# Attention fills of two transformer blocks dealt to other places, and the value product one head later

## The chip, the cores and the metric

The kernel runs on one core of one Trainium2 chip. Its time is the device time of one execution in microseconds. Three runs of the kernel before took 2408.8 to 2412.59 us, with a median of 2411.03 us. Everything below about waits and durations comes from one further execution that a hardware profiler recorded.

## The reference: two blocks over 512 tokens

The input is 512 tokens of width 1024. Block 1 conditions on a vector `c`, runs two kinds of attention side by side, and then looks experts up; block 2 is a transformer layer with 16 extra tokens. Everything is float32. Cut to what the change touches:

```python
def first_block(...):                      # DEPTH = 1
    mod = (silu(c) @ w_ada + b_ada).reshape(b, 6, d)         # six rows of 1024
    shift1, scale1, gate1, shift2, scale2, gate2 = ...
    hn = rmsnorm(x, norm1_g) * (1 + scale1) + shift1
    qa, ka, va, qi, ki, wi, qb, kb, vb, ga, gb = split(hn @ w_in)
    ya = dsa_attention(qa, ka, va, qi, ki, wi, rel_bias)     # 8 heads, top 128 keys by an index score, bias by distance
    yb = stick_breaking_attention(qb, kb, vb)                # 8 heads
    merged = sigmoid(ga) * (ya @ w_proj_a) + sigmoid(gb) * (yb @ w_proj_b)
    x = x + gate1 * (merged @ w_out)
    hn2 = rmsnorm(x, norm2_g) * (1 + scale2) + shift2
    x = x + gate2 * peer_ffn(hn2, ...)
    return rmsnorm(x, final_g)

def _layer(...):                           # block 2
    a_out = forgetting_attention(q, k, v, cum_logf)          # 8 heads
    p_out = pooled @ w_pool * pool_scale                     # 4 groups
    h = h + concat(a_out, p_out) @ w_out
    n2 = rmsnorm(h, norm2_w)
    return h + (silu(n2 @ w_gate) * (n2 @ w_up)) @ w_down
```

## The kernel before

Each float32 product is built from three products of rounded parts: every operand is split into a high part and the remainder, and `mm3` (L177 to L179) issues high by high, low by high, and high by low. A weight chunk is loaded by one 512 KB transfer on the queue SP (`raw`, L168), copied to `whi` on ScalarE (L171) and subtracted to `wlo` on VectorE (L172). Every split on VectorE is one subtraction (`hilo`, L243, L246).

The program text is handed to a framework that puts each engine's instructions into one order from its own estimate of when they are ready; an engine then works through its order and waits at the first instruction whose inputs are missing. The order of the text therefore matters less than where an item is offered, and a tile's memory can be given to its next user only when the last reader is done.

Block 1's attention has two stages. In the first (pool `pb`) the eight stick-breaking heads run: `sb_z` computes a head's scores and softplus parts, `sb_t` multiplies them with a triangular matrix (L645, L646) and leaves the weights `ah` and `al`, and `pv` multiplies these with the values (L413, L414), after which `head_sum` (L447, L448) adds the parts into `yb`. In the second (pool `pa`) the eight index-selected heads run: `da_s` with the softmax (L762 to L766), `transpose_p` (TensorE transposes L777, split into `pth` and `ptl`), and `pv` and `head_sum` again, into `ya`. Before these two stages an index stage forms the score tiles `iacc1` to `iacc3`.

Other work is dealt into 32 slots, two per head, by the table `B1F`: slots 0 to 15 belong to the first stage, 16 to 31 to the second. One letter is one item:

- `k`: a query or key projection for one pair of heads: 24 matmuls of 512 columns, one `whi`, one `wlo`, and two split subtractions (`dup`, `stk`).
- `g`: a gate projection: 24 matmuls, one `whi`, one `wlo`.
- `v`: the value projection of the second stage: 192 matmuls of 256 columns, four `wlo`, eight small split subtractions.
- `t`: a step of the top-128 search, alternately `MAX8` and `MATCH_REPLACE8` on `iacc` (L592, L593).
- `a`: half of one of the rows of `silu(c) @ w_ada` that are not needed at the start. Four transfers of 512 KB (`adaraw`, L300, in two buffers) are multiplied by the condition and summed by eight VectorE instructions into `adaacc` (L286, L288). A matmul with a vector of ones then sums over partitions (L305, the tile is 128x512 and the matmul is float32, which appears as two matmul records), VectorE adds a bias row (L308), for two of the eight halves also scales it (L311), and a 2 KB transfer writes the row to `modrow` in DRAM (L312).

The bias table of the second stage is made between the index stage and the first heads: `rb` and `oh` are loaded (L542, L543), multiplied (L547), negated into `rs` (L548), written to DRAM (`rdr`, L549) and spread to `r128` (L551). These tiles lie in a pool `pr` that opens when the index stage's pool closes.

After the heads come `w_proj_a` and `w_proj_b` (eight column blocks, 406 to 496 us), `w_out` with the second normalisation (to about 570 us), then the expert part, which the change does not touch. Block 2's eight heads (1890 to 1990 us) have a table of their own, `B2F`, of eleven slots; its letters are column blocks of the u projection (a to d), pooling sums (e to h), pooling products (A to D), the second half of q and v, and four blocks of the pooled half of `w_out` (W to Z). Its `w_out` for the attention half runs row block by row block; after each of four, `done` adds it to `x`, normalises (`xn`, L1452) and transposes it into `n2h` and `n2l` (`rows_out`, L235). The feed-forward starts with `gemm_halves`: four products over the first 256 tokens, then over the last 256.

Of the kernel before, what the change touches and what calls it, by code (L numbers as in the profile page):

```python
# [11 lines left out]
F32 = mybir.dt.float32  # L12
# [15 lines left out]
H = 8  # L28
# [43 lines left out]
class Kern:  # L72
# [207 lines left out]
    def ada_acc(self, acc, raws, cond):  # L280
        nc = self.nc
        for kc in range(0, KC, 2):
            raw = raws(kc)
            for j in range(2):
                if kc + j == 0:
                    nc.vector.tensor_scalar(acc, raw[:, 0], cond[:, 0:1], None, op0=ALU.mult)  # L286
                else:
                    nc.vector.scalar_tensor_tensor(acc, raw[:, j], cond[:, kc + j:kc + j + 1], acc,  # L288
                                                   op0=ALU.mult, op1=ALU.add)

    def ada(self, pool, cond, col, dst_row, half, gain=None):
        nc, I = self.nc, self.I
        wv = I["w_ada"].rearrange("(k p) n -> p k n", p=128)
        if True:
            c0 = col * D + half * 512

            def raws(kc):
                raw = pool.tile([128, 2, 512], F32, tag="adaraw", bufs=ADB, name=self.nm("adaraw"))
                with self.tc.issue_after(self.loaded):
                    nc.sync.dma_start(raw, wv[:, kc:kc + 2, c0:c0 + 512])  # L300
                return raw
            acc = pool.tile([128, 512], F32, tag="adaacc", bufs=1, name=self.nm("adaacc"))
            self.ada_acc(acc, raws, cond)
            p = self.psg()
            nc.tensor.matmul(p, lhsT=self.onesf, rhs=acc, start=True, stop=True)  # L305
            bro = pool.tile([1, 2, 512], F32, tag="adab", bufs=1, name=self.nm("adab"))
            nc.sync.dma_start(bro[:, 0], I["b_ada"][0:1, c0:c0 + 512])
            nc.vector.tensor_tensor(bro[:, 0], p[0:1], bro[:, 0], op=ALU.add)  # L308
            if gain is not None:
                nc.sync.dma_start(bro[:, 1], I[gain][0:1, half * 512:half * 512 + 512])  # L310
                nc.vector.scalar_tensor_tensor(bro[:, 0], bro[:, 0], 1.0, bro[:, 1], op0=ALU.add, op1=ALU.mult)  # L311
            nc.sync.dma_start(self.modrow[dst_row:dst_row + 1, half * 512:half * 512 + 512], bro[:, 0])  # L312
# [143 lines left out]
    def block1(self):  # L456
# [40 lines left out]
        with tc.tile_pool(name="pidx", bufs=1) as pi:  # L497
            pva = pat_ctx.enter_context(tc.tile_pool(name="pva", bufs=1, side="right"))
            pad = pat_ctx.enter_context(tc.tile_pool(name="pad", bufs=1, side="right"))
            adas = fillers([(lambda c=c, r=r, g=g, hf=hf: self.ada(pad, cond, c, r, hf, g))  # L500
                            for c, r, g in ((2, 0, None), (4, 1, "norm2_g"), (3, 2, None), (5, 3, None)) for hf in range(2)])
# [19 lines left out]
            acc = {b: b1.tile([128, 128 * (b + 1)], F32, name=f"iacc{b}") for b in range(1, 4)}  # L521
            for pr in range(4):
# [58 lines left out]
        fill = {"g": fillers([gate_fill(n, j) for n in range(4) for j in range(2)]), "a": adas, "v": va_fill,  # L581
# [29 lines left out]


# [23 lines left out]
        def sb_t(pool, st):  # L636
            zs, sph, spl = st
            ahs, als = [], []
            for s in range(TB):
# [9 lines left out]
                ah = pool.tile([128, n], F32R, tag=f"ah{s}", name=self.nm("ah"))  # L649
                al = pool.tile([128, n], F32R, tag=f"al{s}", name=self.nm("al"))  # L650
# [6 lines left out]
        with tc.tile_pool(name="pb", bufs=1) as pb:  # L657
            cur = sb_z(pb, 0)
            for h in range(H):
                fills(2 * h)  # L660
                nxt = None
# [931 lines left out]
```

## Time and profile before

| | |
|---|---|
| median of three runs | 2411.03 us (2408.8 to 2412.59) |
| profiled execution, its own time | 2410.34 us |
| span from the first to the last instruction | 2408.5 us |
| TensorE busy / VectorE busy / ScalarE busy | 96% / 72% / 43% |
| mean granted TensorE clock, share of full speed | 0.981 |
| chain that ended last: TensorE / VectorE / DMA / ScalarE | 86% / 7% / 2% / 2% |

The span is 1.84 us shorter than the execution's own time; that remainder lies around it and is taken as fixed. A busy share is a mean over stages that differ, so the rows below are cut by stage. TensorE's busy time contains stretches at the lower of its two clock levels (1.2 instead of 2.4 GHz), where the same matmul takes twice as long; the column PEclk shows the mean over the stretch. What TensorE loses in a stretch is therefore its idle time plus (1 minus PEclk) times the stretch.

### The profile page before, as it was taken

The numbers are of one execution on the slowest core, as the hardware profiler recorded it, in microseconds if no ns is written. First come the engines' busy times: TensorE is split into PE (matmuls) and PEld (weight loads), VectorE is DVE, ScalarE is ACT, GpSimd is POOL, SyncE is SP. The second block draws the span as 40 slices with busy tenths as digits, with TensorE's granted clock in tenths as the row PEclk, the third lists the DMA queues.
The fourth block names the chain that finished last, engine by engine and source line by source line (L and its number), as shares of the span: only waits on it lengthen the run. The fifth ranks groups of instructions, "written<-read, shape, count | busy, mean of one in ns | idle before, by whom it ended". The sixth has DMA issues, their size and how long they took to land.

```text
span 2408.5 us, 34258 instructions
## 1 busy us (share of the span) xinstructions
PE 2320.4 (96%) x12409; PEld 2020.5 (84%) x12409; DVE 1745.1 (72%) x3461; ACT 1038.6 (43%) x1698; POOL 375.1 (16%) x286
## 2 busy tenths in 40 slices
PE   7899888999999999999999999999999989999999
PEld 6777776888899899999999988888888878888887
DVE  7698958466999898885788898878886786333321
ACT  3466545343345566654333333333354563322211
POOL 0000000000002133541443452222200000000000
PEclk9999999999999999999999999999999999999999
DMA  9353644462245699999999999999952413333231
GB/s 264 107 140 98 174 114 133 121 197 83 88 151 180 215 348 356 351 348 326 329 322 341 328 362 350 338 359 348 361 198 67 102 49 97 96 96 91 93 114 44
DMA packets 309870, 498.69 MB, mean 207 GB/s; under 512 B 22514, under 2 KB 204402, under 8 KB 308164
## 3 DMA queue, kind: packets, MB, share of 16 engines
q1 hardware_dynamic: 270916, 355.97, 45.0%
q0 software_dynamic: 38784, 140.53, 16.7%
q8 instruction: 97, 1.59, 0.3%
q14 instruction: 73, 0.60, 0.1%
HBM read 444.98 MB, written 47.76 MB: 205 GB/s over the span
## 4 chain that ended last, share of the span: by engine, by line
PE 86%; DVE 7%; DMA 2%; ACT 2%; issue 1%; SPq 0%; DVEq 0%; ACTq 0%
PE a L177 17%; PE a L178 17%; PE a L179 17%; PE g L177 10%; PE g L178 10%; PE g L179 10%; PE g L952 2%; DMA adaraw<-in_w_ada_dram 1%; DVE wlo L172 1%; ACT whi L171 1%; DMA raw<-in_u_t_dram 1%; DVE ptl L243 1%; DVE adaacc L288 1%; PE g L414 0%; PE a L777 0%
## 5 line engine op out<-in xcount | busy, mean ns | idle before, releaser
L172 DVE TENSOR_TENSOR wlo<-raw,whi 128x1024 fp32r<-128x1024 f32 x425 | 518.4, 1223 | 352.3 <-ACT whi L171 348.8
L171 ACT ACTIVATE whi<-raw 128x1024 fp32r<-128x1024 f32 x425 | 445.9, 1055 | 618.7 <-PE g L178 328.0
L177 PE MATMUL g<-nh,whi 128*128 128x512 f32 (+4 forms) x1024 | 385.3, 376 | 7.1 <-DVE yb L448 3.3
L178 PE MATMUL g<-nl,whi 128*128 128x512 f32 (+4 forms) x1024 | 383.8, 375 | 0.0
L179 PE MATMUL g<-nh,wlo 128*128 128x512 f32 (+4 forms) x1024 | 382.0, 373 | 0.0
L177 PE MATMUL a<-nh,whi 128*128 128x384 f32 (+2 forms) x912 | 308.1, 345 | 8.5 <-ACT whi L171 5.9
L178 PE MATMUL a<-nl,whi 128*128 128x384 f32 (+2 forms) x912 | 310.3, 340 | 1.4 <-DVE nl L243 1.4
L179 PE MATMUL a<-nh,wlo 128*128 128x384 f32 (+2 forms) x912 | 307.6, 339 | 0.4 <-DVE wlo L172 0.4
L178 PE MATMUL a<-wlo,ch 128*128 128x512 f32 x768 | 299.2, 390 | 0.0
L179 PE MATMUL a<-whi,cl 128*128 128x512 f32 x768 | 298.8, 389 | 0.0
L1026 POOL DMA_INDIRECT raw<-in_u_dram,eidx x128 | 172.4, 1347 | 739.9 <-DVE eidx L1014 384.6
L177 PE MATMUL a<-whi,ch 128*128 128x512 f32 x768 | 281.3, 390 | 1.4 <-ACT whi L171 1.4
L1026 POOL DMA_INDIRECT raw<-in_v_dram,eidx x128 | 188.5, 1472 | 269.3 <-DVE gacc L1039 127.6
L177 PEld LDWEIGHTS g<-nh,whi 128*128 128x128 f32 (+1 forms) x1024 | 193.3, 189 | 39.1 <-DVE yb L448 3.7
L179 PEld LDWEIGHTS g<-nh,wlo 128*128 128x128 f32 (+1 forms) x1024 | 193.5, 189 | 29.4 <-issue 0.2
L178 PEld LDWEIGHTS g<-nl,whi 128*128 128x128 f32 (+1 forms) x1024 | 193.4, 189 | 29.3
L242 ACT ACTIVATE ch<-cf 128x384 fp32r<-128x384 f32 x128 | 67.2, 525 | 297.3 <-PE a L178 188.5
L177 PEld LDWEIGHTS a<-nh,whi 128*128 128x128 f32 x912 | 175.5, 193 | 12.9 <-ACT whi L171 7.1
L178 PEld LDWEIGHTS a<-nl,whi 128*128 128x128 f32 x912 | 175.4, 192 | 4.3 <-DVE nl L243 1.8
L179 PEld LDWEIGHTS a<-nh,wlo 128*128 128x128 f32 x912 | 175.2, 192 | 3.1 <-DVE wlo L172 0.8
L177 PEld LDWEIGHTS a<-whi,ch 128*128 128x128 f32 x768 | 144.1, 188 | 30.3 <-ACT whi L171 1.8
L179 PEld LDWEIGHTS a<-whi,cl 128*128 128x128 f32 x768 | 144.2, 188 | 29.9
(394 smaller groups left out, 3987.1 us busy)
## 6 DMA issues: line engine op xcount, KB each, us to landing
raw<-in_u_t_dram SPq DMA_DIRECT2D x128, 512.0 KB
raw<-in_v_dram SPq DMA_DIRECT2D x128, 512.0 KB
raw<-in_w_in_dram SPq DMA_DIRECT2D x54, 512.0 KB
gdr<-gblk SPq DMA_DIRECT2D x12, 2048.0 KB
vg<-gdr SPq DMA_DIRECT2D x384, 64.0 KB
udr<-ug SPq DMA_DIRECT2D x44, 384.0 KB
vu<-udr SPq DMA_DIRECT2D x44, 384.0 KB
adaraw<-in_w_ada_dram SPq DMA_DIRECT2D x32, 512.0 KB
```

What stands on the lines that cost most here:

```text
L171: nc.scalar.activation(hi, raw, AF.Copy)
L172: nc.vector.tensor_tensor(lo, raw, hi, op=ALU.subtract)
L177: mm(out, lhsT=lh, rhs=rh, start=start, stop=False, skip_group_check=skip)
L178: mm(out, lhsT=lh, rhs=rl, start=False, stop=False, skip_group_check=skip)
L179: mm(out, lhsT=ll, rhs=rh, start=False, stop=stop, skip_group_check=skip)
L242: nc.scalar.activation(hi, src, AF.Copy)
L243: r = nc.vector.tensor_tensor(lo, src, hi, op=ALU.subtract)
L288: nc.vector.scalar_tensor_tensor(acc, raw[:, j], cond[:, kc + j:kc + j + 1], acc, op0=ALU.mult, op1=ALU.add)
L952: nc.tensor.matmul(p[:, ts(j, 128)], lhsT=s2[:, c], rhs=rep[k][:, c // 2, :, c % 2], start=(i == 0), stop=(i == 1))
L1026: nc.gpsimd.indirect_dma_start(out=u, out_offset=None, in_=I[src], in_offset=bass.IndirectOffsetOnAxis(ap=eidx[:, i:i + 1], axis=0))
```

## The change

1. A new function `heads` runs both attention stages. It issues `pv` and `head_sum` of head h-1 behind the second step of head h. `ah`, `al`, `pth` and `ptl` get two buffers each.
2. `B1F` is dealt anew, with `v` at slot 15 instead of 17. A top-128 step is 4 pairs of instructions instead of 6, and the table has enough of them in the first stage.
3. `a` is parted into `a` (loads and the eight VectorE instructions) and `r` (matmul, bias row, write), two slots later. The sum is kept in `iacc3`, which the top-128 search has finished with; the next sum reuses it. No `a` is left in slots 0 to 15: five are in 16 to 31, three in a new table `WPF` beside `w_proj`.
4. The bias table's loads come at the head of the index stage and its arithmetic ahead of the index loop; the pool `pr` is gone.
5. `gt`, `a2`, `s2` (the rows read back for the second normalisation) move to a pool that opens later.
6. Row block 3 of block 2's second normalisation goes to `late`: its transposes are issued between the two halves of the feed-forward's first products, and its `xn` lies in a buffer of the `raw` ring.
7. `B2F` is dealt anew: the four W to Z blocks are spread over three slots instead of two, and u blocks, v and pooling items shift by a slot.

```diff
-B1F = ('kk', 'g', 't', 'gkktt', '', 'ga', 't', '', '', 'gtkg', 'kt', 'a', 'kgak', 'k', '', '', 'a', 'v', 'ka', '', 'kk', '', 'k', 'a', '', 'kg', '', 'a', '', 'ga', '', '')
-ADB = 2
+B1F = ('kk', 'gt', 'kt', 'kt', 'gt', 't', 'kt', 'kt', 'gt', 't', 'kt', 'kt', 'gt', 'gt', 't', 'v',
+       'ka', 'k', 'r', 'gka', '', 'kr', 'a', 'gk', 'r', 'ka', '', 'gr', 'a', '', 'r', '')
+WPF = ('', 'a', '', 'ra', '', 'ra', '', 'r')
-TG = 6
+TG = 4
-B2F = ('', 'ba', 'f', 'q', 'ev', 'cdg', 'h', 'CA', 'DB', 'W', 'YZX')
+B2F = ('', 'b', 'af', 'q', 'ec', 'dg', 'v', 'hCA', 'DBW', 'XY', 'Z')
...
-    def gemm_halves(self, chunks, xh, xl, outs):
+    def gemm_halves(self, chunks, xh, xl, outs, between=()):
         for c in (slice(0, 256), slice(256, 512)):
+            for f in between if c.start else ():
+                f()
...
+    def ada(self, pool, acc, cond, col, dst_row, half, gain=None):
...
+        def row():
             p = self.psg()
             nc.tensor.matmul(p, lhsT=self.onesf, rhs=acc, start=True, stop=True)
...
+            nc.vector.tensor_tensor(acc[0:1], p[0:1], bro, op=ALU.add)
...
+            nc.sync.dma_start(self.modrow[dst_row:dst_row + 1, half * 512:half * 512 + 512], acc[0:1])
+        return row
...
+            rb = pva.tile([32, 8], F32, name="rb")
+            oh = pva.tile([32, 640], F32, name="oh")
+            rs = pva.tile([8, 640], F32, name="rs")
+            nc.sync.dma_start(rb, I["rel_bias"])
+            nc.sync.dma_start(oh, I["bucket"])
...
+        def heads(f0, first, second, v, y):
+            def out(h, ph):
+                self.head_sum(self.pv(v, h, *ph), y[:, h // 2], h % 2)
+
+            cur, done = first(0), None
+            for h in range(H):
+                fills(f0 + 2 * h)
+                nxt = None
+                if h + 1 < H and (h + 1) % 2:
+                    nxt = first(h + 1)
+                ph = second(cur)
+                if done is not None:
+                    out(h - 1, done)
+                if h + 1 < H and not (h + 1) % 2:
+                    nxt = first(h + 1)
+                fills(f0 + 2 * h + 1)
+                cur, done = nxt, ph
+            out(H - 1, done)
...
-                fills(2 * h + 1)
-                self.head_sum(self.pv(vb, h, ph[0], ph[1]), yb[:, h // 2], h % 2)
...
-                fills(17 + 2 * h)
-                self.head_sum(self.pv(va["v"], h, ph[0], ph[1]), ya[:, h // 2], h % 2)
...
+            for c in WPF[n]:
+                fill[c]()
...
-        gt = prw.tile([128, D], F32, name="gt")
+        gt = prm.tile([128, D], F32, name="gt")
...
-            self.rows_out(n2h, n2l, 128 * t, xn)
+            if t < 3:
+                self.rows_out(n2h, n2l, 128 * t, xn)
+            else:
+                late.append(lambda: self.rows_out(n2h, n2l, 128 * t, xn))
```

How the change moves instructions, at three places. First, TensorE near the end of the second stage, before. L777 is a transpose of a head's weights (from which `pth` and `ptl` are split), L413 and L414 are the value product; `pth_3886` is the split of the bank `a_3879`.

```order
L777 MATMUL a_3879<-cst,P_3766 128x128
L777 MATMUL a_3880<-cst,P_3766 128x128
L777 MATMUL a_3881<-cst,P_3766 128x128
L305 MATMUL g_3957<-adaacc_3940,onesf 128x512
L413 MATMUL g_3963<-pth_3886,v_2874 128x512
L414 MATMUL g_3963<-ptl_3887,v_2874 128x512
```

And the same head now, where L772, L410 and L411 are these three lines and `pth_3848` is the split of `a_3841`:

```order
L772 MATMUL a_3842<-cst,P_3705 128x128
L772 MATMUL a_3887<-cst,P_3837 128x128
L772 MATMUL a_3887<-cst,P_3827 128x128
L772 MATMUL a_3887<-cst,P_3817 128x128
L772 MATMUL a_3888<-cst,P_3827 128x128
L772 MATMUL a_3888<-cst,P_3817 128x128
L772 MATMUL a_3889<-cst,P_3817 128x128
L772 MATMUL a_3887<-cst,P_3807 128x128
L772 MATMUL a_3888<-cst,P_3807 128x128
L772 MATMUL a_3889<-cst,P_3807 128x128
L300 MATMUL g_3881<-iacc_1002,onesf 128x512
L410 MATMUL g_3916<-pth_3848,v_2564 128x512
```

The transposes of the next head (`a_3887` to `a_3889`) now stand between a head's transposes and its product. Counted in rows from a bank's last transpose to the first product of its head, the eight heads stood at 112, 40, 6, 36, 31, 7, 4 and 4 before and stand at 8, 68, 42, 85, 30, 36, 17 and 13 now.

Second, VectorE. Before, a stretch in the first stage: sums of `a` (L288) among the top-128 search (L592, L593) and the split and softplus steps of the heads (L243, L628).

```order
L288 SCALAR_TENSOR_TENSOR adaacc_2417<-adaraw_2418,cond,adaacc_2417 128x512
L593 MATCH_REPLACE iacc_997<-m_2_1845,iacc_997 128x384
L243 TENSOR_TENSOR al_2261<-sbt_2258,ah_2260 128x128
L288 SCALAR_TENSOR_TENSOR adaacc_2417<-adaraw_2422,cond,adaacc_2417 128x512
L592 MAX m_2_1845<-iacc_997 128x8
L628 SCALAR_TENSOR_TENSOR sbt_2270<-a_2264,sbt_2270 128x512
L288 SCALAR_TENSOR_TENSOR adaacc_2417<-adaraw_2422,cond,adaacc_2417 128x512
```

And now, the second sum, in the second stage (L294 and L296 are the sum's two lines, `iacc_1002` is `iacc3`):

```order
L294 TENSOR_SCALAR iacc_1002<-adaraw_3192,cond 128x512
L296 SCALAR_TENSOR_TENSOR iacc_1002<-adaraw_3192,cond,iacc_1002 128x512
L296 SCALAR_TENSOR_TENSOR iacc_1002<-adaraw_3196,cond,iacc_1002 128x512 x2
L296 SCALAR_TENSOR_TENSOR iacc_1002<-adaraw_3200,cond,iacc_1002 128x512 x2
L445 TENSOR_TENSOR ya<-g_3068,ya 64x512
L296 SCALAR_TENSOR_TENSOR iacc_1002<-adaraw_3204,cond,iacc_1002 128x512
L246 TENSOR_TENSOR ptl_3047<-a_3039,pth_3046 128x512
```

No sum stands in the first stage any more. In the second they stand in runs: here six of eight follow each other with nothing between, and the third transfer (`adaraw_3200`) can start only when the first buffer has been read.

Third, VectorE at the start of block 2's feed-forward, before: `nl` of row block 0 (from the banks `g_20104` and `g_20111`) and what stands ahead of it.

```order
L172 TENSOR_TENSOR wlo_20307<-raw_20304,whi_20306 128x1024
L172 TENSOR_TENSOR wlo_20313<-raw_20310,whi_20312 128x1024
L257 SCALAR_TENSOR_TENSOR rq_20206<-rh_20204,rr_20205 128x1
L1449 TENSOR_TENSOR x<-x,a_20228 128x512
L1449 TENSOR_TENSOR x<-x,a_20229 128x512
L172 TENSOR_TENSOR wlo_20319<-raw_20316,whi_20318 128x1024
L261 SCALAR_TENSOR_TENSOR rr_20205<-rq_20206,rr_20205 128x1
L172 TENSOR_TENSOR wlo_20528<-raw_20525,whi_20527 128x1024
L243 TENSOR_TENSOR nl_20038<-g_20104,nh_20037 128x4x128
```

And now (L246 is that `nl`, L1447 the scaling to `xn`, L173 the `wlo` subtraction):

```order
L1447 SCALAR_TENSOR_TENSOR xn_3663_20143<-x,rr_20136,n2w 128x1024
L1447 SCALAR_TENSOR_TENSOR xn_3673_20198<-x,rr_20191,n2w 128x1024
L246 TENSOR_TENSOR nl_20024<-g_20090,nh_20023 128x4x128
L256 TENSOR_SCALAR rh_20245<-ss_20242 128x1
L246 TENSOR_TENSOR nl_20024<-g_20097,nh_20023 128x4x128
L260 SCALAR_TENSOR_TENSOR rq_20247<-rh_20245,rr_20246 128x1
L264 SCALAR_TENSOR_TENSOR rr_20246<-rq_20247,rr_20246 128x1
L1447 SCALAR_TENSOR_TENSOR raw_20253<-x,rr_20246,n2w 128x1024
L246 TENSOR_TENSOR nl_20024<-g_20145,nh_20023 128x4x128
L246 TENSOR_TENSOR nl_20024<-g_20152,nh_20023 128x4x128
L173 TENSOR_TENSOR wlo_20273<-raw_20270,whi_20272 128x1024
```

Four `wlo` subtractions of the feed-forward's first chunks stood ahead of row block 0's `nl`; now all of them stand behind `nl` of blocks 0 and 1.

On SP the loads of the bias table moved to the start of the index stage, and four loads of `peer_wq` chunks that stood ahead of the last `w_out` chunks now stand directly behind the store of `hn2d` (L793).

## Rows read from the trace of the kernel before

**Rows 1.** The page: busy time by engine, and the chain's shares.

```profile
PE 2320.4 (96%) x12409; PEld 2020.5 (84%) x12409; DVE 1745.1 (72%) x3461; ACT 1038.6 (43%) x1698; POOL 375.1 (16%) x286
...
PE 86%; DVE 7%; DMA 2%; ACT 2%; issue 1%; SPq 0%; DVEq 0%; ACTq 0%
```

**Rows 2.** Busy time of stretches, with granted clock (PEclk).

```profile
core 0: us, PE busy (x) PEld busy (x) DVE busy (x) ACT busy (x) POOL busy (x), PEclk, DMA share, GB/s
104.00:296.00 192.00, 169.84 (x858) 136.39 (x856) 177.83 (x389) 123.91 (x282) 4.08 (x8) 0.95 0.48 138
296.00:406.00 110.00, 96.13 (x480) 76.60 (x479) 76.39 (x195) 48.35 (x116) 3.19 (x6) 0.93 0.50 137
406.00:496.00 90.00, 89.70 (x378) 72.16 (x379) 40.41 (x51) 31.60 (x44) 0.00 (x0) 0.98 0.35 103
545.00:570.00 25.00, 20.43 (x130) 19.36 (x131) 15.55 (x25) 9.76 (x18) 0.00 (x0) 0.80 0.27 78
1890.00:1990.00 100.00, 90.41 (x615) 79.14 (x614) 77.90 (x216) 55.40 (x136) 2.04 (x4) 0.91 0.22 59
```

**Rows 3.** The same view, three shorter stretches.

```profile
131.00:168.00 37.00, 36.25 (x181) 29.85 (x180) 33.78 (x70) 25.79 (x57) 1.02 (x2) 1.00 0.53 153
168.00:210.00 42.00, 38.04 (x184) 30.63 (x183) 40.02 (x101) 32.55 (x78) 1.02 (x2) 0.92 0.41 112
360.00:406.00 46.00, 38.98 (x191) 29.87 (x190) 39.90 (x109) 24.01 (x63) 1.02 (x2) 0.96 0.58 161
```

**Rows 4.** That view, instructions on the tile adaacc alone.

```profile
104.00:296.00 192.00, 4.24 (x8) 1.29 (x8) 28.30 (x40) 0.95 0.48 138
296.00:406.00 110.00, 4.20 (x8) 1.22 (x8) 17.06 (x24) 0.93 0.50 137
```

**Rows 5.** The tile adaacc: ns min/median/max, first and last start.

```profile
L288 DVE SCALAR_TENSOR_TENSOR adaacc<-adaraw,cond,adaacc x56: 721/748/753, 113.9 to 392.3; 128x512 f32<-128x512 f32 x56
```

**Rows 6.** The same view of the tile adab.

```profile
L308 DVE TENSOR_TENSOR adab<-g,adab x8: 668/670/679, 187.4 to 395.1; 1x512 f32<-1x512 f32 x8
```

**Rows 7.** What TensorE waited for, 104 to 296 us (total us, times, longest).

```profile
PE g L547 <- DMA oh<-in_bucket_dram: 3.4, 1, 3.4
PE g L177 <- DVE yb L448: 3.3, 2, 2.7
```

**Rows 8.** The same, 296 to 406 us.

```profile
PE a L777 <- DVE ptl L243: 3.0, 1, 3.0
PE g L414 <- DVE ptl L243: 2.4, 3, 1.1
...
PE g L413 <- DVE v L243: 2.1, 1, 2.1
PE g L413 <- DVE adab L308: 1.8, 1, 1.8
```

**Rows 9.** Waits of VectorE, 104 to 406 us.

```profile
DVE adaacc L288 <- DMA adaraw<-in_w_ada_dram: 6.8, 6, 2.7
```

**Rows 10.** Waits of the DMA queue SP, 104 to 406 us.

```profile
SPq L307 <- DMA modrow<-adab: 5.8, 5, 2.3
```

**Rows 11.** The chain of waits, 360 to 400 us: start us, us, what.

```profile
364.45 3.96 DMA adaraw<-in_w_ada_dram
...
376.53 6.64 DMA adaraw<-in_w_ada_dram
```

**Rows 12.** The timeline at the feed-forward's start: start us, us, engine, line.

```profile
2033.08 1.23 DVE L172 TENSOR_TENSOR wlo<-raw,whi 128x1024 fp32r<-128x1024 f32 x1
...
2034.22 1.29 DVE L243 TENSOR_TENSOR nl<-g,nh 128x512 fp32r<-128x512 f32 x2
...
2034.96 1.36 PE L235 MATMUL g<-cst,xn 128*128 128x128 f32 x8 [3.72 <-DVE nl L243]
```

**Rows 13.** The timeline at the end of block 1's norm, queue SP.

```profile
557.01 0.33 SPq L793 DMA_DIRECT2D hn2d<-hn2t  x1
```

**Rows 14.** The same on TensorE.

```profile
562.22 0.58 PE L177 MATMUL a<-nh,whi 128*128 128x256 f32 x1 [1.83 <-ACT nh L242]
```

More of the change, by code (lines that the diff above doesn't have):

```diff
@@ L284, in ada_acc @@
             for j in range(2):
-                if kc + j == 0:
+                k = kc + j
+                if k == 0:
                     nc.vector.tensor_scalar(acc, raw[:, 0], cond[:, 0:1], None, op0=ALU.mult)
                 else:
[L288 to L303, printed above, removed]
+                    nc.vector.scalar_tensor_tensor(acc, raw[:, j], cond[:, k:k + 1], acc, op0=ALU.mult, op1=ALU.add)
@@ L309, in ada @@
             if gain is not None:
[L310 to L312 removed]
+                bro = pool.tile([1, 512], F32, tag="adab", bufs=1, name=self.nm("adab"))
+                nc.sync.dma_start(bro, I[gain][0:1, half * 512:half * 512 + 512])
@@ L521, in block1 @@
             acc = {b: b1.tile([128, 128 * (b + 1)], F32, name=f"iacc{b}") for b in range(1, 4)}
+            for j, (a0, n) in enumerate(((0, 512), (512, 128))):
+                p = self.psg()
+                nc.tensor.matmul(p[:8, :n], lhsT=rb, rhs=oh[:, a0:a0 + n], start=True, stop=True)
+                nc.vector.tensor_scalar(rs[:, a0:a0 + n], p[:8, :n], -1.0, None, op0=ALU.mult)
+            nc.sync.dma_start(rdr, rs)
+            for h in range(H):
+                nc.sync.dma_start(r128[h], rdr[h:h + 1].broadcast_to([128, 640]))
             for pr in range(4):
@@ L580, in block1 @@
                 qks += [qk_fill(pat, "q" + kind, pr, c0, scale), qk_fill(pat, "k" + kind, pr, c0 + 512, None)]
-        fill = {"g": fillers([gate_fill(n, j) for n in range(4) for j in range(2)]), "a": adas, "v": va_fill,
+        fill = {"g": fillers([gate_fill(n, j) for n in range(4) for j in range(2)]), "v": va_fill,
                 "k": fillers(qks[2:])}
@@ L657, in block1 @@
         with tc.tile_pool(name="pb", bufs=1) as pb:
[L658 to L661, printed above, removed]
-                if h + 1 < H and (h + 1) % 2:
-                    nxt = sb_z(pb, h + 1)
-                ph = sb_t(pb, cur)
-                if h + 1 < H and not (h + 1) % 2:
-                    nxt = sb_z(pb, h + 1)
-                fills(2 * h + 1)
-                self.head_sum(self.pv(vb, h, ph[0], ph[1]), yb[:, h // 2], h % 2)
-                cur = nxt
+            heads(0, lambda h: sb_z(pb, h), lambda st: sb_t(pb, st), vb, yb)
         vb_ctx.close()
@@ L689, in da_s @@
             return pt
+        pad = ctx.enter_context(tc.tile_pool(name="pad", bufs=1))
+        adas = [(c, r, hf, g) for c, r, g in ((2, 0, None), (4, 1, "norm2_g"), (3, 2, None), (5, 3, None)) for hf in range(2)]
+        rows = []
+        fill["a"] = lambda: rows.append(self.ada(pad, acc[3], cond, *adas.pop(0)))
+        fill["r"] = lambda: rows.pop(0)()
         pya = ctx.enter_context(tc.tile_pool(name="pya", bufs=1))
@@ L693, in block1 @@
         with tc.tile_pool(name="pa", bufs=1) as pa:
-            cur = da_s(pa, 0)
-            for h in range(H):
-                fills(16 + 2 * h)
-                nxt = None
-                if h + 1 < H and (h + 1) % 2:
-                    nxt = da_s(pa, h + 1)
-                ph = self.transpose_p(pa, cur)
-                if h + 1 < H and not (h + 1) % 2:
-                    nxt = da_s(pa, h + 1)
-                fills(17 + 2 * h)
-                self.head_sum(self.pv(va["v"], h, ph[0], ph[1]), ya[:, h // 2], h % 2)
-                cur = nxt
+            heads(16, lambda h: da_s(pa, h), lambda st: self.transpose_p(pa, st, 2), va["v"], ya)
         pat_ctx.close()
@@ L1470, in block2 @@
                 ps = [self.psa() for _ in range(4)]
-                self.gemm_halves([self.split_chunk(w[:, :, ts(f, 128)]) for f in range(2) for w in (wg, wu)], n2h, n2l, ps)
+                self.gemm_halves([self.split_chunk(w[:, :, ts(f, 128)]) for f in range(2) for w in (wg, wu)], n2h, n2l, ps, late)
                 for f in range(2):
```

54 lines of the change are left out of this document (21 added, 33 removed).

## The prediction

> **What bounds the kernel now.** I began with the page's busy times and the chain: TensorE is busy for 96% of the span and holds 86% of the chain, VectorE 7% [rows 1]. A gain can thus come only from stretches in which TensorE idles or runs at its lower clock level. I looked for them next in the view of stretches [rows 2]. What TensorE loses is its idle time plus (1 - PEclk) times the length. Stick-breaking stage, 104 to 296 us: 192 - 169.8 = 22.2 idle and 0.05 x 192 = 9.6 of clock, 31.8 us together, 17% of the stage. Second stage, 296 to 406 us: 13.9 + 7.7 = 21.6 us. `w_proj`, 406 to 496 us: 0.3 + 1.8 = 2.1 us. Block 2's heads, 1890 to 1990 us: 9.6 + 9.0 = 18.6 us. The reader should see beside it what VectorE does: it is busy for 177.8 of 192 us (93%) in the first stage, 76.4 of 110 (69%) in the second, 40.4 of 90 (45%) in `w_proj`.
>
> A full VectorE alone does not make TensorE lose: 131 to 168 us has VectorE at 91% and TensorE losing 0.75 us of 37 (2%); 168 to 210 us has 95% and a loss of 4.0 + 3.4 = 7.4 us (17%); 360 to 406 us has 87% and a loss of 7.0 + 1.8 = 8.8 us (19%) [rows 3]. What differs is whether TensorE's next item needs something that is queued on VectorE. The view of waits names such things: `yb` (the sum behind `pv`), `ptl`, `v`, `adab` [rows 7, 8].
>
> **The change, part by part.** A fill `k` or `g` is 24 matmuls; 378 matmuls take 89.7 us in `w_proj` [rows 2], 0.238 each, so a fill is 5.7 us of TensorE. `v`, 192 matmuls of half the columns, is 22.8 us. One sum of `a` is 28.30 us / 5 = 5.7 us of VectorE (40 instructions in the first stage, 24 in the second, so five sums and three) [rows 4, 5]. Its matmul pair costs 4.24/4 = 1.06 us of TensorE, its bias row 0.67 us of VectorE [rows 4, 6].
>
> *First stage.* Five sums and their bias rows leave VectorE: 28.3 + 5 x 0.67 = 31.7 us. One `k` and one `g` leave too (8 `k` now, 9 before; 5 `g`, 6 before): 11.4 us of TensorE, and on VectorE two `wlo` of 1.23 us [rows 12] and two split subtractions of about 0.67, 3.8 us. `v` comes in: 22.8 us of TensorE; four `wlo` and eight small subtractions on VectorE, by the same rows some 8 us. VectorE then has 177.8 - 31.7 - 3.8 + 8.2 = 150.5 us; TensorE, without its losses, 160.2 + 11.4 = 171.6 us. VectorE is no longer the fuller one. What share will TensorE lose? Ends: 2%, as in 131 to 168 us, and 17%, as now. The sums stood ahead of `al` and the softplus steps that TensorE waits for, and they go; the in-order queue and the chain inside a head stay. I take 8%, the middle: 171.6 / 0.92 = 186.5 us. Less the 11.4 us of work moved in, that compares as 175.1 with 192: **-16.9 us** (ends -28 and +2). In it is the bias table: TensorE waits 3.4 us for `oh` [rows 7], whose load now lies far ahead.
>
> *Second stage.* Two more sums with bias rows, 12.7 us; one more `k` and `g`, 3.8 us; `v` gone, -8.2 us: VectorE 76.4 + 8.3 = 84.7 us. TensorE: 110 - 21.6 + 11.4 - 22.8 = 77.0 us. Here VectorE becomes the fuller engine. At 90% (between 87% of 360 to 406 us and 93% of the first stage) the stage takes 94.1 us; with the 11.4 us that went to the first it compares as 105.5 with 110: **-4.5 us** (at 95%: -9; at 85%: +1). The product one head later removes waits of the kind `ptl` (3.0 and 2.4 us), and with `v` earlier its 2.1 us go [rows 8]; what is late next is VectorE itself. Only head 0's product still stands close behind its own transposes.
>
> *`w_proj`.* Three sums, 3 x 6.4 = 19.2 us of VectorE, lie beside TensorE, which has VectorE at 45% there. TensorE pays the three matmul pairs, 3 x 1.06 = **+3.2 us**, which the two stages above are already rid of. Ends: 0, and 8.6 if each also brings the 1.8 us wait that `adab` once cost [rows 8].
>
> *Block 2's heads.* The deal moves items by a slot and spreads W to Z; no instruction goes. At stake are 18.6 us [rows 2]. Between nothing and 12 us I take a third, **-6.2 us**: block 1's best stretches show that even placing can halve such a loss, and half of this table is unchanged.
>
> *Feed-forward.* TensorE waits 3.72 us for a bank that `nl` of row block 0 frees; `nl` starts at 2034.22 us, just when the last `wlo` ahead of it ends [rows 12]. Not block 3's transposes but VectorE's queue held it. The new order puts those `wlo` behind `nl` of blocks 0 and 1, which helps; but the first GEMM's second product needs the first of them, so the wait moves there. I take **0** (ends -3.7 and +2.5).
>
> *Norm.* Four `peer_wq` loads now go behind the store of `hn2d`, which was issued at 557.0 us [rows 13]. TensorE meets a wait of 1.83 us for `nh` at 562.2 us anyway [rows 14] and then has a half of `gemm_halves` before it needs them, some 11 us (96 matmuls of 0.119). Loads of this size took 4 to 6.6 us [rows 11]. **0** (ends -2 and +5). `gt`, `a2`, `s2` later: hidden by `w_out`.
>
> Sum: -16.9 - 4.5 + 3.2 - 6.2 = -24.4 us. The profiled execution took 2410.34 us, of which 1.84 lie outside the span; that is 0.7 under the median of the runs, so no correction is needed. 2410.3 - 24.4 = 2386 us.
>
> **Rivals.** *Latency, not load, holds the first stage.* The loss share stays at 17% because each head's own chain sets it, and only the bias table's wait (3.4 us) and, by my estimate, a third of the stage's 9.6 us of clock go, -6.5; second stage -4.5, `w_proj` +3.2, block 2 -3: 2399 us. For it: 168 to 210 us, where the loss is 17% although two stretches with equal VectorE load differ eightfold. Against: a sum of 5.7 us in front of a head's steps is a latency too.
>
> *Everything fits.* First stage at its end of -28, second -9, `w_proj` +3, block 2 -12, feed-forward -3.7: 2360 us. For it: `w_proj` runs with a loss of 2% once work is even. Against: both stages stay over 80% full on VectorE.
>
> *Slower: the sums stall VectorE in the second stage.* Five sums stand there in runs, with two load buffers, and each sum's first instruction must wait until the row before it, now kept in `iacc3`, is written out. Two loads of a sum can start only behind the buffer's reader. Loads on the chain took 3.96 and 6.64 us [rows 11], mean 5.3, against 1.5 us of work per buffer: 2 x 3.8 = 7.6 us, and 2.3 us for the write, the longest such wait [rows 10], 9.9 us per sum, 50 us for five. VectorE's instructions behind a waiting sum are `ptl` and the softmax, for which TensorE waits. The second stage would be +45, the whole +25: 2435 us. It decides from about 5 us per sum (24.4 / 5). Against: eight sums before waited 6.8 us in six waits, 0.85 us per sum, the longest 2.7 [rows 9].
>
> The Trainium skill speaks for this rival (page "SBUF — State Buffer", section "The DMA setup-cost knee"): every transfer pays about 2 us that do not shrink with its size, mostly until completion is known, and the rest goes by bytes at 436 GB/s. The 2.3 us that SP waited for a 2 KB write agrees [rows 10]; for 512 KB the page gives 3.2 us (an estimate from its fit), less than the two loads of [rows 11]. By it a stalled sum would cost 2 x (3.2 - 1.5) + 2 = 5.4 us, five of them 27 us, which would eat the forecast gain almost exactly.
>
> *It only moves the losses.* Idle time leaves one slot and returns in the next, as a deal of the same work can do; only the 6.5 us of the bias table less 3.2 remain: 2407 us.
>
> **How the numbers follow.** Forecast 0.47 (its own range 2374 to 2398), latency 0.19, everything fits 0.12, stalled sums 0.11, losses moved 0.11. The predicted time is the forecast's, 2386 us. For 8 in 10 I leave out stalled sums, half of "everything fits" and a little of "losses moved": 2362 to 2409 us. This kernel's runs tell apart about 0.2%, 5 us. Faster than 2406 us: 0.47 + 0.19 + 0.12 = 0.78, less 0.02 for the latency case's upper end, 0.76. Within: "losses moved" and that 0.02, less 0.01 that goes beyond, 0.12. Slower: 0.12.
>
> **What would show it.** Right: no idle time of TensorE for `oh`; between 120 and 290 us VectorE near 80% and TensorE's loss under 10%; fewer `ptl` waits; VectorE near 90% in the second stage, waiting under 2 us per sum for `adaraw`; the three `w_proj` sums beside TensorE at 98%. Wrong: a first stage still at 17%, waits for `adaraw` or for the row's write over 5 us per sum, or a new wait of TensorE for `whi` after 570 us (the moved `peer_wq` loads).

## The result and the profile after

The changed kernel takes 2439.49 us (median of 4 runs, 2437.97 to 2440.84), the kernel before 2410.70: a ratio of 1.0124, 95% interval 1.0112 to 1.0136. It is slower by 29 us where 24 us less was forecast. The profiled execution took 2440.84 us over a span of 2438.7 us.

On the page the shares of the chain have moved: TensorE from 86% to 79%, VectorE from 7% to 9%, DMA from 2% to 6% [rows 1].

```profile
PE 2328.7 (95%) x12405; PEld 2023.7 (83%) x12409; DVE 1747.7 (72%) x3461; ACT 1037.2 (43%) x1698; POOL 385.5 (16%) x286
...
PE 79%; DVE 9%; DMA 6%; issue 3%; ACT 2%; POOL 1%; SPq 1%; DVEq 0%; POOLq 0%; ACTq 0%
```

The view of stretches of the changed kernel, where its stages now lie: first stage to 280 us, second to 404, `w_proj` to 500, a piece of the expert part, and block 2's heads [rows 2].

```profile
core 0: us, PE busy (x) PEld busy (x) DVE busy (x) ACT busy (x) POOL busy (x), PEclk, DMA share, GB/s
104.00:280.00 176.00, 165.09 (x894) 136.71 (x895) 144.89 (x325) 120.46 (x270) 4.10 (x8) 0.97 0.34 86
280.00:404.00 124.00, 99.82 (x441) 76.59 (x443) 98.06 (x239) 56.05 (x134) 3.07 (x6) 0.86 0.58 165
404.00:500.00 96.00, 96.00 (x408) 76.56 (x407) 57.48 (x76) 32.83 (x44) 0.00 (x0) 1.00 0.52 158
1200.00:1450.00 250.00, 234.12 (x1112) 206.83 (x1111) 181.77 (x220) 76.87 (x107) 107.25 (x79) 0.97 0.85 289
1914.00:2014.00 100.00, 86.14 (x583) 75.79 (x582) 73.96 (x205) 52.67 (x129) 2.05 (x4) 0.89 0.22 61
```

The same piece of the expert part in the kernel before:

```profile
1200.00:1450.00 250.00, 248.62 (x1228) 223.31 (x1227) 211.88 (x254) 88.33 (x122) 118.50 (x90) 1.00 0.95 339
```

The reader should see the fourth of the five rows beside this one. In 250 us of a part in which no line of the program was changed, the profile has 1228 matmuls before and 1112 now; DMA fell from 339 to 289 GB/s; VectorE, whose instructions are the same in this part, was busy 30 us less. How long VectorE waited there for gathered rows, after and then before (total us, times, longest):

```profile
DVE gjunk L1027 <- DMA raw<-in_u_dram,eidx: 35.2, 15, 5.4
DVE gacc L1034 <- DMA raw<-in_v_dram,eidx: 32.1, 15, 5.8
```

```profile
DVE gacc L1039 <- DMA raw<-in_v_dram,eidx: 1.7, 2, 1.1
DVE gjunk L1032 <- DMA raw<-in_u_dram,eidx: 1.7, 3, 1.0
```

Before, VectorE idled there too, but mostly for copies that ScalarE makes, and TensorE waited for 1.4 us in all:

```profile
DVE wlo L172 <- ACT whi L171: 18.7, 27, 2.2
DVE cl L243 <- ACT ch L242: 14.5, 15, 1.7
PE a L177 <- ACT whi L171: 1.4, 1, 1.4
```

`gjunk` and `gacc` are the sums over gathered rows: each takes one row per token, for one block of 128 tokens (the other three blocks are computed densely). TensorE, after, same stretch, waits for what stands behind them on VectorE:

```profile
PE a L179 <- DVE wlo L173: 13.0, 5, 3.5
PE g L180 <- DVE wlo L173: 2.7, 3, 1.4
```

The order of the instructions suggests why; experiment 5 tests it. The program text of this part is the same in both, but the framework dealt VectorE's instructions otherwise. With tiles matched (a number after is 14 less than before), `wlo` of chunk `raw_12396` stood directly behind the sum over gather `raw_12393`; now it stands behind the sum over a gather three later. From the 190th to the 250th `wlo` of the program, one to four more gather sums stand ahead of each than before, 2.1 on the mean. Counted in the same way, experiments 1 and 4 below have the order of the changed kernel, 7 nearly so (1.9 more), 5 has 1.9 fewer than before, and all the others have the order of before but for two places at most.

```
before: gacc<-raw_12390, gacc<-raw_12393, wlo_12399<-raw_12396, gacc<-raw_12458, ...
after (numbers of before): gacc<-raw_12461, cf, gacc<-raw_12527, wlo_12399<-raw_12396, gacc<-raw_12530, ...
```

To place the difference I count every matmul at the usual distance of its form (the time from its start to the next one's) and compare when two kernels have done the same work. The table gives us against the kernel before, one execution each, at the work that it had done at the time on top; a negative number means earlier:

| | 296 | 360 | 406 | 570 | 1200 | 1450 | 1890 | 2030 | end |
|---|---|---|---|---|---|---|---|---|---|
| changed | -15.7 | -18.7 | -1.6 | -5.0 | -8.8 | +23.9 | +22.7 | +27.9 | +30.2 |
| gt pool alone | 0.2 | 0.8 | 1.5 | -4.3 | -8.1 | +19.3 | +16.6 | +16.3 | +15.6 |
| steps of 5 | -18.0 | -20.1 | -4.2 | -5.3 | -5.2 | -5.1 | -5.1 | -2.1 | 0.2 |
| bias late | -16.8 | -15.5 | -3.6 | -7.0 | -7.8 | -7.8 | -7.9 | -4.4 | -2.3 |
| deal 2 old | -17.2 | -18.1 | -1.7 | -4.6 | -8.2 | +19.2 | +16.5 | +15.9 | +17.1 |
| gathers held | -16.3 | -18.4 | -2.8 | -5.9 | -8.2 | -2.7 | -3.7 | -0.5 | 1.9 |
| attention alone | -20.5 | -23.0 | -7.5 | -8.5 | -8.2 | -8.1 | -8.2 | -8.1 | -8.6 |
| quarter sums | -18.1 | -25.4 | -20.4 | -22.9 | -27.0 | +1.1 | -1.5 | 1.6 | 0.9 |
| gates in tail | 0.2 | 3.0 | 3.0 | -1.0 | -3.0 | -3.0 | -2.3 | -1.9 | -2.5 |
| three sums | -20.1 | -22.3 | -12.6 | -14.3 | -15.9 | -15.9 | -15.2 | -14.8 | -15.3 |
| two sums | -20.3 | -21.2 | -17.9 | -21.0 | -23.1 | -23.1 | -23.2 | -23.2 | -23.3 |

Executions of one kernel spread by more than 5 us (the kernel before 2403.35 to 2414.35 us in the 23 runs beside experiments 9 to 12, experiment 11 2410.59 to 2425.23), so a small difference in a single column says little.

### The profile page after: what moved, and what is told of

It is laid out like the page before. It is cut to its first block, busy times and chain, and to the rows that moved or that the text cites. A ratio compares the mean times of both kernels' runs of the same rounds, so it can differ in the third digit from the quotient of the medians.

```text
span 2438.7 us, 34256 instructions
## 1 busy us (share of the span) xinstructions
PE 2328.7 (95%) x12405; PEld 2023.7 (83%) x12409; DVE 1747.7 (72%) x3461; ACT 1037.2 (43%) x1698; POOL 385.5 (16%) x286
## 3 DMA queue, kind: packets, MB, share of 16 engines
q0 software_dynamic: 38784, 140.53, 16.9%
## 4 chain that ended last, share of the span: by engine, by line
PE 79%; DVE 9%; DMA 6%; issue 3%; ACT 2%; POOL 1%; SPq 1%; DVEq 0%; POOLq 0%; ACTq 0%
PE a L179 16%; PE a L180 16%; PE a L178 16%; PE g L178 8%; PE g L179 8%; PE g L180 8%; DMA raw<-in_v_dram,eidx 2%; PE g L947 1%; DVE wlo L173 1%; DMA raw<-in_u_dram,eidx 1%; DMA raw<-in_u_t_dram 1%; DMA adaraw<-in_w_ada_dram 1%; DVE m L584 1%; POOL raw L1021 1%; DVE iacc L585 1%
## 5 line engine op out<-in xcount | busy, mean ns | idle before, releaser
L173 DVE TENSOR_TENSOR wlo<-raw,whi 128x1024 fp32r<-128x1024 f32 x425 | 517.4, 1220 | 310.7 <-ACT whi L172 304.3
L178 PE MATMUL a<-whi,ch 128*128 128x512 f32 x768 | 301.5, 395 | 4.5 <-ACT whi L172 4.5
L1021 POOL DMA_INDIRECT raw<-in_u_dram,eidx x128 | 179.1, 1399 | 742.7 <-DVE eidx L1009 390.0
L1034 DVE SCALAR_TENSOR_TENSOR gacc<-raw,gpre,gacc 128x1024 f32<-128x1024 f32 x127 | 162.6, 1281 | 34.0 <-DMA raw<-in_v_dram,eidx 32.4
L1027 DVE CUSTOM_DVE_ANT_0 gjunk<-raw,hn2g 128x1024 bf16<-128x1024 f32 x128 | 156.3, 1221 | 42.6 <-DMA raw<-in_u_dram,eidx 41.8
L179 PEld LDWEIGHTS a<-wlo,ch 128*128 128x128 f32 x768 | 146.8, 191 | 45.0 <-DVE wlo L173 15.3
```

The costliest lines, as they stand in the source:

```text
L173: nc.vector.tensor_tensor(lo, raw, hi, op=ALU.subtract)
L178: mm(out, lhsT=lh, rhs=rh, start=start, stop=False, skip_group_check=skip)
L179: mm(out, lhsT=lh, rhs=rl, start=False, stop=False, skip_group_check=skip)
L1021: nc.gpsimd.indirect_dma_start(out=u, out_offset=None, in_=I[src], in_offset=bass.IndirectOffsetOnAxis(ap=eidx[:, i:i + 1], axis=0))
L1027: nc.vector.tensor_tensor_reduce(junk, u, hn2, 1.0, 0.0, ALU.mult, ALU.add, pre[:, i:i + 1])
L1034: nc.vector.scalar_tensor_tensor(acc, v, pre[:, i:i + 1], acc, op0=ALU.mult, op1=ALU.add)
```

## The experiments

**1. gt pool alone.** Before, with one edit:

```diff
-        gt = prw.tile([128, D], F32, name="gt")
+        gt = prm.tile([128, D], F32, name="gt")
         (a2 and s2 likewise; the pool prw goes)
```

> The kernel before with one edit: gt, a2 and s2 lie in the pool prm instead of prw. No instruction goes or comes. Theory (order of the expert part): this edit alone gives VectorE and SP in the expert part the order that the changed kernel has there, with the gather sums up to three places earlier among the wlo subtractions; then VectorE waits for gathers, wlo comes late and TensorE starves between 1200 and 1500 us: 2411 + 22 to 35 = 2433 to 2446 us, and VectorE waits over 40 us for gathered rows. Rival (the attention's new deal shifts transfers into the expert part, or its sums delay it): the attention is untouched here, so 2408 to 2415 us, and VectorE waits under 5 us for gathered rows.

2429.99 us (2425.93 to 2437.57), ratio 1.0091 (1.0069 to 1.0112). Most of the slowdown returns with an untouched attention. VectorE waits 36.7 and 27.9 us for gathered rows between 1200 and 1450 us:

```profile
1200.00:1450.00 250.00, 232.34 (x1124) 205.82 (x1124) 183.47 (x222) 76.96 (x107) 107.89 (x79) 0.99 0.86 291
```

The time lies 3 us under the range I gave; the mechanism is the one expected.

**2. Steps of 5.** The changed kernel with

```diff
-TG = 4
+TG = 5
```

> The changed kernel with one constant of the top-128 search: 5 pairs of instructions per step instead of 4. Everything else of the change stays. Theory (order of the expert part): the framework then orders the expert part as it did before, so the loss there goes: 2439 - 26 to 36 = 2403 to 2413 us. Rival (the attention's deal itself or the later loads slow the expert part): the change is all there, so 2435 to 2443 us.

2409.78 us, ratio 0.9993 (0.9983 to 1.0002): as fast as before, and the stretch of the expert part reads as before:

```profile
1200.00:1450.00 250.00, 248.62 (x1226) 222.99 (x1225) 212.39 (x254) 87.35 (x120) 114.23 (x89) 1.00 0.95 341
```

**3. Bias late.** The changed kernel, the bias table's loads and arithmetic back behind the index stage, in a pool of their own.

> The changed kernel with the bias table's loads and arithmetic back behind the index stage. Theory (order of the expert part): here too the expert part has the order of before, so the loss there goes, and what the early table saved in the attention (TensorE's wait of 3.4 us and some clock, 2 to 7 us) comes back: 2406 to 2418 us. Rival (deal or loads slow the expert part): 2441 to 2446 us, later than the changed kernel by the table's wait.

2410.44 us, ratio 1.0012 (1.0000 to 1.0023). The expert part is as before. That the early table saves anything is not seen: this kernel ends with the one of experiment 2.

**4. Deal 2 old.** The changed kernel with `B2F` of before.

> The changed kernel with block 2's old deal. The expert part keeps the order of the changed kernel. If the new deal costs time (block 2's heads and w_out lost 3.7 us against before in the profiles): 2434 to 2437 us. If it is neutral and the loss is of one execution: 2438 to 2441 us. If the deal gains as predicted (6 us): 2444 to 2447 us.

2429.08 us, ratio 1.0085 (1.0067 to 1.0103), some 10 us under the changed kernel and 5 us under the lowest of the three ranges, so none of them holds. In the table the expert part cost 27 us here and 33 there; between 1890 and 2030 us this kernel loses nothing where the changed one loses 5. The sign is that of the first range: the new deal costs time.

**5. Gathers held.** The changed kernel; each gather's sum may be ordered only behind the last `wlo` issued before it in the text:

```diff
-        nc.vector.tensor_tensor(lo, raw, hi, op=ALU.subtract)
+        self.lastlo = nc.vector.tensor_tensor(lo, raw, hi, op=ALU.subtract).ins
...
+            with tc.issue_after(self.lastlo):
                 nc.vector.tensor_tensor_reduce(junk, u, hn2, ...)
         (the sum into gacc likewise)
```

> The changed kernel, but each sum over gathered rows on VectorE may be ordered only behind the wlo subtraction of the chunk issued before it; attention, block 2 and feed-forward stay as changed. Theory (VectorE's order is what starves TensorE: a gather's sum stands ahead of a wlo and waits for its transfer): the loss between 1200 and 1450 us goes, 2405 to 2417 us, and VectorE waits under 15 us for gathered rows. Rival (the order of SP's loads, or the transfers themselves, are late in the changed kernel, and VectorE only shows it): TensorE still loses over 20 us there, 2428 to 2442 us.

2414.63 us, ratio 1.0023 (1.0008 to 1.0039). 25 of the 29 us are back, and VectorE no longer waits for gathered rows in that stretch:

```profile
1200.00:1450.00 250.00, 244.71 (x1198) 218.82 (x1197) 209.17 (x247) 84.32 (x117) 121.13 (x86) 0.99 0.95 331
```

In every other experiment the order of SP's transfers in the expert part goes with VectorE's; in this kernel it is that of neither the kernel before nor the changed one, so it is VectorE's order that counts, as far as one experiment can tell the two apart. What is left in the table, 5.5 us between 1200 and 1450 us, holds one wait of TensorE for `whi` of 4.9 us.

**6. Attention alone.** The changed kernel with steps of 5, `B2F` of before and row block 3 back in `done`.

> The changed kernel with top-128 steps of 5, block 2's old deal, and row block 3 of the second normalisation back in its old place: what is left of the change is block 1's attention, in an expert part ordered as before. Theory (attention gains 5 us at 570 us, block 2's new deal costs 3 to 5, the late transposes 1 to 2): 2410 - 5 = 2403 to 2407 us. Rival (deal 2 and late transposes cost nothing, their differences are noise of one execution): as with steps of 5 alone, 2408 to 2412 us.

2400.25 us, ratio 0.9957 (0.9941 to 0.9973): the attention's part of the change, with steps of 5, is a gain of 9 us in an expert part ordered as before, and the time lies 3 us under the theory's range.

**7. Quarter sums.** As 6, with `for kc in range(0, 2, 2)` in `ada`; three quarters of each sum are left out.

> As the attention alone, but each sum of a takes only the first quarter of its terms: three of four loads and six of eight VectorE instructions are left out. Its expert part has the slow order, so the time at the end of the norm (570 us in the kernel before) is what counts. Theory (the second stage lost its forecast gain because its last heads have too little TensorE work beside their own chain): the last 60 us of the second stage still lose over 14 of the 19 us that TensorE lost there against equal work. Rival (the sums stall VectorE, as priced before): those stalls go and the second stage ends 12 us or more earlier than with full sums.

2411.34 us (one run, with the changed kernel's kind of order in the expert part, though its steps are of 5). At the work of 406 us it stands at -20.4 us where experiment 6 stands at -7.5, and at 570 us at -22.9 against -8.5: three quarters of the sums cost 13 us up to the second stage's end and 14 us up to 570 us. My theory of empty slots fails: between 360 and 406 us of work this kernel loses 5 us where experiment 6 loses 16. The rival's 12 us are there. Whether it is the sums' time on VectorE or their wait for loads, this run does not tell, as both are left out. The second stage with full sums (experiment 6) and with a quarter:

```profile
280.00:400.00 120.00, 95.88 (x424) 73.48 (x423) 95.13 (x227) 54.30 (x128) 3.10 (x6) 0.87 0.55 158
```

```profile
280.00:388.00 108.00, 92.60 (x439) 71.29 (x438) 77.06 (x204) 56.59 (x132) 3.13 (x6) 0.95 0.37 100
```

**8. Gates in the tail.** As 6, with `g` out of slots 8, 12 and 13 and the late slots `'ka'` (19), `'g'` (26), `'ag'`, `'g'`, `'rg'` (28 to 30).

> As the attention alone, with three gate projections moved from the first stage (slots 8, 12, 13) to the last slots of the second (26, 29, 30, and one from 19 to 28), in an expert part ordered as before. Theory (too little TensorE work in the last slots): TensorE's idle and low clock there are filled, 5 to 14 us less than the attention alone: 2391 to 2400 us. Rival (VectorE with its sums sets the second stage's end): the projections only add their wlo there, and the first stage, poorer in fills, loses nothing or a little: 2403 to 2412 us.

2408.94 us, ratio 1.0000 (0.9989 to 1.0010): the whole gain of the attention is gone, and the time lies in the rival's range, but neither account holds whole. The two stages, cut where the last head of the first ends, here and then in experiment 6:

```profile
104.00:268.00 164.00, 148.95 (x796) 122.42 (x794) 138.21 (x312) 111.96 (x257) 4.08 (x8) 0.93 0.30 75
268.00:405.00 137.00, 117.79 (x520) 90.27 (x520) 103.48 (x247) 57.07 (x134) 3.10 (x6) 0.91 0.60 170
```

```profile
104.00:272.00 168.00, 158.54 (x869) 131.15 (x867) 141.37 (x315) 116.96 (x263) 4.08 (x8) 0.98 0.32 82
272.00:395.00 123.00, 99.47 (x449) 76.77 (x449) 97.16 (x241) 53.28 (x130) 3.10 (x6) 0.89 0.58 170
```

In the second stage TensorE lost 31.5 us here and 37.1 there (idle time and clock), so the gates fill about 6 us of it, the low end of the theory. But the first stage, which by the rival should lose nothing or a little, lost 26.5 us against 12.8: the fills were needed there.

**9 and 10. Three sums, two sums.** As 6, with sums moved from the second stage's late slots to `w_proj`:

```diff
-       'ka', 'k', 'r', 'gka', '', 'kr', 'a', 'gk', 'r', 'ka', '', 'gr', 'a', '', 'r', '')
-WPF = ('', 'a', '', 'ra', '', 'ra', '', 'r')
+       'ka', 'k', 'r', 'gka', '', 'kr', '', 'gk', '', 'k', '', 'g', '', '', '', '')
+WPF = ('a', 'ra', 'ra', '', 'ra', 'ra', 'ra', 'r')
```

(that is 10, with steps of 4; 9 keeps an `a` at slot 22 and has steps of 5).

> The attention alone, with two more sums of a moved from the second stage to beside w_proj: three stay in the second stage (slots 16, 19, 22), five lie beside w_proj. The expert part has the order of before. Theory (each sum costs the second stage 2.9 us, by the quarter sums, and less beside w_proj, where VectorE is at 58%): 2400 - 2 to 6 = 2394 to 2398 us. Rival (five sums, 72 of 90 us of VectorE with the rest, stall w_proj's own splits): 2400 to 2406 us.

> As three sums, but two in the second stage and six beside w_proj, with steps of 4; the expert part has the order of before. Theory: 2400 - 3 to 9 = 2391 to 2397 us. Rival (w_proj becomes the stage that VectorE sets): later than with three sums, 2400 to 2408 us.

2396.80 us, ratio 0.9939 (0.9926 to 0.9953), and 2393.73 us, ratio 0.9931 (0.9917 to 0.9946). Both lie in the theory's ranges, and both beat the kernel before (by under 1%, but clear of the noise) and the changed one; the intervals do not part the two. `w_proj` with six sums:

```profile
390.00:482.00 92.00, 92.00 (x388) 72.70 (x387) 68.80 (x94) 30.34 (x42) 0.00 (x0) 1.00 0.69 210
```

VectorE is at 75% and TensorE has no gap: the sums are free there but for their matmul pairs.

**11 and 12. Deal 2 alone, late transposes alone**, each on the kernel before.

> The kernel before with block 2's new deal and nothing else; the expert part has the order of before. Theory (the new deal costs 3 to 5 us, as in the profiles that have it): 2412 to 2415 us against 2409 to 2410. Rival (as predicted, a gain of some 6): 2402 to 2406 us. No effect: 2408 to 2411 us.

> The kernel before with row block 3's transposes late and nothing else. Theory (the wait only moves): 2409 to 2412 us, TensorE idle for 3 to 5 us at the feed-forward's start as before. Rival (the wait goes): 2405 to 2407 us.

Experiment 11: 2416.50 us, ratio 1.0027 (1.0016 to 1.0039): the new deal of block 2 costs 6 us, 1.5 us over the range I gave. Experiment 12: 2412.75 us, ratio 1.0005 (0.9996 to 1.0014): the late transposes do nothing that can be measured.

## Why the prediction was wrong

**The expert part** is the step that failed. The prediction followed each edit to its own place and took the expert part, "which the change does not touch", at nothing. There the profiled execution lost 33 us (table, 1200 to 1450 us; 29 from 570 us on, as it was 4 us quicker before that stretch), the whole difference of 30, and the quoted order shows what to look for: text that is the same, dealt otherwise. The edits to `gt`'s pool, the step of the top-128 search and the bias table each flip it: experiment 1 flips it on, 2 and 3 off. The step itself is no rule: experiment 7 has steps of 5 and the new order, 10 steps of 4 and the old one. VectorE works through its order, so a gather's sum whose row has not landed holds the `wlo` behind it, and TensorE waits for that. Loads and gathers share one ring of `raw` buffers, so a held VectorE would also free them late; DMA's fall from 339 to 289 GB/s fits that, but no run took it apart. Why so small an edit tips the framework's estimate was not settled.

That the changed kernel lost 33 us there and experiments 1, 4 and 7 27 to 28 is mostly the clock. At the same work (1200 to 1450 us of before) the changed kernel and experiment 1 read:

```profile
1191.00:1474.00 283.00, 262.62 (x1230) 230.65 (x1229) 208.99 (x251) 87.70 (x121) 121.25 (x89) 0.96 0.86 295
1192.00:1469.00 277.00, 256.10 (x1226) 225.67 (x1225) 206.32 (x246) 85.40 (x119) 120.50 (x89) 0.98 0.87 298
```

TensorE idles for 20.4 and 20.9 us (18.6 and 19.5 in experiments 4 and 7), but the granted clock costs 0.04 x 283 = 11 us in the one and 0.02 x 277 = 6 us in the other. Why the clock was lower with the same idle time is open.

**First stage, -16.9 us forecast.** Right: -15.7 us at 296 us of work. Between 104 and 280 us TensorE lost 10.9 us idle and 0.03 x 176 of clock, 9% where I took 8%; no wait for `oh` is left, and that for `yb` [rows 7] is 2.4 us:

```profile
PE g L178 <- DVE yb L445: 2.4, 2, 1.5
```

That the bias table's early load is part of this gain, as I wrote, is not shown: experiment 3 waits 2.6 us for `oh` again and still has -16.8.

The cut at 296 us was wrong, though. In the kernel before, the last head's sum in `yb` starts at 279.9 us, so 16 us of what I called the first stage belong to the second:

```profile
L448 DVE TENSOR_TENSOR yb<-g,yb x8: 665/688/696, 160.3 to 279.9; 64x512 f32<-64x512 f32 x8
104.00:280.00 176.00, 156.87 (x750) 123.74 (x749) 162.45 (x348) 115.94 (x260) 4.08 (x8) 0.95 0.47 131
280.00:405.00 125.00, 109.01 (x589) 89.16 (x587) 91.04 (x233) 55.35 (x135) 3.19 (x6) 0.93 0.53 148
```

By this cut the first stage lost 27.9 us before (16%) and 16.2 us now (9%), so the reading stands.

**Second stage, -4.5 us forecast.** Wrong: +14 us, from -15.7 to -1.6. By the right cut TensorE lost 24.7 of 125 us there before and 41.5 of 124 us now. My sum for VectorE started from 76.4 us where the stage already held 91.0, which explains most of the gap between its 84.7 us and the measured 98.1. And I took VectorE at 90% full; it was at 79% (98.1 of 124 us) with TensorE at 81%. Neither was full, and each waited for the other. The waits that answer to [rows 8] and [rows 9], 280 to 404 us for TensorE and 104 to 500 us for VectorE:

```profile
PE a L410 <- DVE st L757: 4.1, 3, 1.7
PE g L300 <- DVE iacc L296: 3.7, 2, 2.9
PE a L772 <- DVE P L761: 3.3, 2, 1.9
PE a L772 <- DVE ptl L246: 2.9, 1, 2.9
PE g L410 <- DVE iacc L303: 2.7, 2, 1.4
PE g L411 <- DVE ptl L246: 2.3, 2, 2.1
```

```profile
DVE iacc L296 <- DMA adaraw<-in_w_ada_dram: 10.7, 11, 2.7
DVE iacc L294 <- DMA modrow<-iacc: 5.3, 3, 2.4
```

The product one head later took `ptl` ahead of it (5.4 us before) down to 5.2 only. The waits for `st` and `P`, the softmax steps on VectorE, grew from 2.2 and 0.2 us to 4.1 and 3.3. New are 6.4 us in which TensorE stands at a sum's matmul (L300) or at the bank that its bias row frees (L303), a wait that the prediction priced for `w_proj` and not here. The rival "the sums stall VectorE" named this mechanism at 9.9 us per sum. By experiment 7, which leaves out three quarters of each, it is 12.9 us for the five sums up to the stage's end, 2.6 each; by experiments 9 and 10, which move two and three whole sums away, 5.1 and 10.4 us, 2.6 and 3.5 each. That is about a third of the price, too little for the rival to decide. That its 2435 us lie close to the measured 2439.49 is luck: five sums cost some 13 to 17 us and not 50, and the rest was lost in the expert part. VectorE's own waits for loads and for the written row are 16.0 us.

The Trainium skill's rule that I weighed there ("SBUF — State Buffer", "The DMA setup-cost knee") made 5.4 us of a stalled sum, an estimate. The runs gave half to two thirds of that. VectorE's wait for the row's 2 KB write was at most 2.4 us in the changed kernel, near the page's 2 us, and at most 3.6 us in experiment 10:

```profile
DVE iacc L293 <- DMA modrow<-iacc: 13.8, 6, 3.6
```

***w_proj*, +3.2 us.** Right: TensorE has no gap there (96.00 of 96 us at a clock of 1.00), so the three sums cost it their matmul pairs, 3.2 us, and no wait. At equal work the stretch from 406 to 496 us is even 1.4 us shorter, as the kernel before lost 2.1 us in it.

**Block 2's heads, -6.2 us.** Wrong in sign: +6 us (experiment 11). I reasoned from what even placing had done in block 1 and read no wait of block 2 that the new deal would remove. In experiment 11 TensorE waits, for instance, 4.2 us for a pooling item's split (`pph`) between 1890 and 2030 us, which is not among the waits of before there (that execution, at 2425.23 us, is the longest of its 12; the changed kernel's has 3.6 us):

```profile
PE g L177 <- ACT pph L242: 4.2, 2, 2.8
```

**Feed-forward, 0.** The time is right, within the noise (experiment 12; +2.3 us in the table from 2030 us on). The reasoning was not: I expected the wait to move to the first product's `wlo`, but TensorE still waits at the transposes of the norm's rows. Where one wait of 3.7 us stood [rows 12], two stand:

```profile
PE g L238 <- DVE rh L256: 3.2, 1, 3.2
PE g L238 <- DVE nl L246: 1.5, 1, 1.5
```

**Norm, 0.** About at its lower end of -2: -3.4 us between 406 and 570 us of work, of which 1.4 are the stretch of `w_proj`. No new wait for `whi` behind the moved `peer_wq` loads was met. Experiment 1 has -5.9 us there, so the later place of `gt`, `a2` and `s2` seems to bring the gain.

## What to carry to other kernels

When a framework orders the instructions, compare the whole order of the changed kernel with that of before, stage by stage, also where the text is the same, and above all on an engine that works in order and has a load's consumer among the steps that others wait for. Work that waits for transfers belongs beside a stage whose own engine is idle enough to take it: the same sums cost the second stage some 3 us each and `w_proj` little beyond their matmul pair. A deal can be judged only when an unrelated flip of the order is held fixed: here a gain of 9 us (experiment 6) lay under a loss of 29. And a stage is cut where its own last instruction stands, as a cut 16 us late put work into the wrong sum.

## What the runs showed that I had not expected

Transfers that keep DMA 95% busy can still fall behind: in the changed kernel, where VectorE is held up for up to 6 us at a time, the same kinds of transfers ran at 289 instead of 339 GB/s and a share of 85%. And idle time costs TensorE clock as well, in the second stage above all: between 340 and 400 us of the changed kernel, where it idles for 15.5 us in pieces of up to 3 us, the granted clock is 0.80 of full speed on the mean:

```profile
340.00:400.00 60.00, 44.49 (x190) 33.91 (x189) 47.65 (x121) 24.10 (x62) 1.02 (x2) 0.80 0.53 146
```
